# Longer product rows, one unit's place in W_out, a fused bias and maximum, and two sums on GpSimd in a decoder trunk

## The chip, the cores and the metric

The kernel runs on one core of a Trainium2 chip, in one launch. The metric is the device time of an execution in microseconds (us), smaller being better.

## What is computed

A decoder trunk of two layers over 256 tokens of width 1024, in float32. Every layer is a pair of half-step SwiGLU feed-forwards (hidden width 2816) around a token mixer, each with a norm before and after it. The mixer is a gated linear recurrence (width 1344) in the first layer and forgetting attention (16 heads of 64) in the second. Cut to what matters here:

```python
f = swiglu(rms_norm(h, ffn1_pre_g[layer]), ...)          # (silu(x @ w_gate) * (x @ w_up)) @ w_down
h = h + 0.5 * rms_norm(f, ffn1_post_g[layer])
hn = rms_norm(h, mix_pre_g[layer])
m = recurrent_block(hn, ...)                             # ends in  (gelu(gate) * rec) @ w_out
#   or, in the second layer, forgetting_attention:
#   logits = q @ k^T + c[q] - c[k], -inf above the diagonal;  p = softmax(logits);  o = p @ v;  m = o @ w_o
h = h + rms_norm(m, mix_post_g[layer])
f = swiglu(rms_norm(h, ffn2_pre_g[layer]), ...)
h = h + 0.5 * rms_norm(f, ffn2_post_g[layer])
```

Between the layers the shared keys, values and the forget gate's cumulative sum are made from h.

## The kernel before

**Tiles.** The tokens are two tiles t of 128 rows. A float32 number is held as the sum of two numbers of TensorE's faster type, `hi` and `lo`, and a product is three: hi by hi, hi by lo, lo by hi. The weights come from HBM in units of 128 x 1024 (`raw`, 5 buffers, by SyncE's queue). ScalarE copies a unit to `whi` (L204) and VectorE subtracts to get `wlo` (L205); both have 9 buffers.

**Products.** In the feed-forwards' gate and up tiles the weights are stationary and the activations move. `still` and `mmj` work on a row: four PSUM banks by some of the eight blocks of 128 of the contraction. With `whi`, TensorE moves `xhi` and `xlo` side by side, 512 columns (L239, "wide"); with `wlo` it moves `xhi` alone, 256 columns (L245, "narrow"). `grouped` collects units until it gives them to `still`: two units, so 16 wide products and 16 narrow ones, twice for a tile's eight blocks. The other matrices (`row_items`: w_down, W_out, w_o) have the tokens stationary or moving in 512 columns, three products for a unit and half of the output (L212, L213, L214; 6 to a unit). `tick` is called between products; it counts down deferred work (`defer`) and lets the planner load and split further units. `state["edge"]` holds back work that was deferred as calm.

**Order.** TensorE's order is as the program is written. The other engines' instructions stand in the order in which a scheduler put them, each engine in a line of its own; work marked as urgent (`high_priority`) is put forward. W_out has 11 units for each token tile; `OUT_ORDER` says which tile's unit is next.

**Norms and residual.** `enter` takes a finished sub-layer of one token tile in two halves of 512 columns: ScalarE squares each (L260, with a sum `ss` for each half), VectorE multiplies by the gain (L323 or L325), GpSimd adds the two sums and a constant (L253) and takes the power -1/2 (L255), and VectorE multiplies by it and adds h (L329). TensorE then turns h (L269), VectorE multiplies by the next gain (L277), and ScalarE (L278) and VectorE (L283) make `xall` of it. `stat` squares h itself, with one sum. The bfb transfer, `triu` and `ones` (L1051 to L1057) are constants for the forget gate, made by GpSimd when W_out ends.

**Attention.** A step of tile t has a group of heads: 4 for t = 0 (128 keys each), 2 for t = 1 (256 keys each), 512 columns either way; so there are 4 groups and 8. `logits` multiplies q and k (L1198), VectorE adds the bias nb (L1207, in PSUM) and takes each head's negative maximum mx (L1209), ScalarE takes the exponential of each head with its sum (L1215, into `pe` in SBUF), and VectorE divides (L1217, L1218). `turn`, two steps later, transposes pe (L1225), and `values` multiplies by v a step after that (L1239, L1246, L1247).

Of the kernel before, what the change touches and what calls it, by code (L numbers as in the profile page):

```python
# [12 lines left out]
AF = mybir.ActivationFunctionType  # L13
ALU = mybir.AluOpType
AX = mybir.AxisListType

P = 128
D = 1024
# [9 lines left out]
EPS = 1e-6  # L28
# [8 lines left out]
NEG = -1e30  # L37
# [10 lines left out]
def trunk_kernel(ctx: ExitStack, tc: tile.TileContext, A: dict, out: bass.AP):  # L48
    nc = tc.nc
# [11 lines left out]
    def nm(s):  # L61
        uid[0] += 1
        return f"{s}_{uid[0]}"
# [24 lines left out]
    def mmbank():  # L88
        return bank("mm", True)
# [13 lines left out]
    def tensor_work(n):  # L103
        pace["t"] += n * 0.445e-3
# [8 lines left out]
    def tick():  # L113
        for p in list(pend):
            p[0] -= 1
            if p[0] < 0 and not (p[2] and state["edge"]):
                pend.remove(p)
                p[1]()
        purse[0] = min(purse[0] + SHARE, SHARE)
        if state["p"] >= OPEN:  # L120
            prepare_next()
        while queue and purse[0] > 0:
            cost, _, fn = queue.pop(0)
            purse[0] -= cost
            fn()
# [101 lines left out]
    def mmj(bs, parts, ks, moving):  # L227

        o, oh = pall, pall[:, :, :S]
        if len(moving(ks[0])[0].shape) == 4:  # L230
            o = o.rearrange("p n (a t b) -> p n a t b", a=2, t=2)
            oh = oh.rearrange("p n (t b) -> p n t b", t=2)
        else:
            o = o.rearrange("p n (a b) -> p n a b", a=2)
        n = len(ks)
        for i, (k, (wh, wl)) in enumerate(zip(ks, parts)):
            tensor_work(2 * S * len(bs))
            for b, w in zip(bs, wh):
                nc.tensor.matmul(o[:, b], w, moving(k)[0], start=k == 0, stop=False)  # L239
            if n > 1 and i % 2 == 1:  # L240
                tick()
        for i, (k, (wh, wl)) in enumerate(zip(ks, parts)):
            tensor_work(S * len(bs))
            for b, w in zip(bs, wl):
                nc.tensor.matmul(oh[:, b], w, moving(k)[1], start=False, stop=k == 7)  # L245
            if i == 1 and n > 2:
                tick()


    def rstd_of(ss, n, f=1.0):  # L250

        v = spool.tile([P, 1], F32, tag="nv", name=nm("nv"))
        nc.gpsimd.tensor_scalar(v, ss[:, 0:1], ss[:, 1:2] if n == 2 else 0.0, D * EPS * f * f, ALU.add, ALU.add)  # L253
        r = spool.tile([P, 1], F32, tag="rstd", name=nm("rstd"), bufs=8)
        nc.gpsimd.tensor_tensor(r, v, mhalf, ALU.pow)  # L255
        return r
# [125 lines left out]
    state = {"p": 0, "a": 0, "b": 0, "edge": False, "look": 99}  # L382
# [4 lines left out]
    def prepare_next(must=False):  # L387

        i = state["p"]
        if not must and i >= state["a"] + state["look"]:  # L390
            return
        if i >= len(items) or i >= WB and done.get(i - WB, 0) < 2:
            assert not must, i
            return
        if i not in landed:
            landed[i] = max(landed.get(i - 1, 4.0) + LOAD, pace["t"] if i < RAW else split_at[i - RAW] + LATE)
        if landed[i] > pace["t"] and not must:
            return
        pace["t"] = max(pace["t"], landed[i])
        split_at[i] = pace["t"] + 1.0  # L400
        units[i] = items[i][0]()
        state["p"] += 1
# [119 lines left out]
    hooks = {}  # L522
# [23 lines left out]
    def grouped(k0, kept, fn):  # L546

        i = len(items)

        def work(t, u):  # L550
            kept.append((i, u))
            if len(kept) < 2 and not hooks and k0 % 4 == 0:
                return [i]
            us = [v for _, v in kept]
            done_ = [j for j, _ in kept]
            del kept[:]
            fn(us, k0 + 2 - 2 * len(us))
            for j in done_[:-1]:
                done[j] = 2
                units.pop(j)  # L560
        return work
# [444 lines left out]
    for p in range(6):  # L1006
# [1 line left out]
    n_rg = len(items)  # L1008
    RG_ORDER = ("0g0 0g1 0g2 0g3 0g4 0g5 0g6 0g7 1g0 1g1 r0 1g2 r1 gw0 1g3 1g4 r2 gw1 1g5 1g6 r3 gw2 1g7 "
                "0g8 0g9 0g10 r4 gw3 r5 1g8 1g9 gw4 1g10 gw5").split()  # L1010
    OUT_ORDER = [0] * 8 + [1] * 4 + [0] * 3 + [1] * 7

    gbox = {}

# [146 lines left out]
    att = {}  # L1161
# [17 lines left out]
    def attention(t):  # L1179

        ap = pools["a"]
        nk = t + 1
        per = 4 // nk
        np_ = per // 2
        w = nk * P
        box = {}
        G = NH // per

        def head(hg, b, j):
            return 2 * (hg * np_ + j) + b  # L1190

        def logits(hg):
            c = 4 + (hg % 2) * 2
            lg = pall[:, c:c + 2, :S]
            for j in range(np_):
                for b in range(2):
                    p = hg * np_ + j
                    nc.tensor.matmul(lg[:, b, j * w:(j + 1) * w], att["q"][t][b * HD:(b + 1) * HD, p, :],  # L1198
                                     kv["kT"][b * HD:(b + 1) * HD, p, :w], start=True, stop=True)
            v = lg.rearrange("p b (j k) -> p j b k", j=np_)  # L1200
            h0 = hg * per
            bias = att["nb"][t][:, h0:h0 + per, :].rearrange("p (j b) k -> p j b k", b=2)
            if np_ == 1:
                v, bias = lg, att["nb"][t][:, h0:h0 + per, :]
            urgent = tc.high_priority()
            urgent.__enter__()
            nc.vector.tensor_tensor(v, v, bias, ALU.add)  # L1207
            mx = spool.tile([P, 4], F32, tag="mx", name=nm("mx"))[:, :per]
            nc.vector.tensor_reduce(mx, lg.rearrange("p b (j k) -> p b j k", j=np_), AX.X, ALU.max, negate=True)  # L1209
            sm = spool.tile([P, 4], F32, tag="sm", name=nm("sm"))[:, :per]  # L1210
            pe = box["pe", hg] = ap.tile([P, per, w], F32, tag="pe", name=nm("pe"), bufs=2)
            for b in range(2):
                for j in range(np_):
                    i = b * np_ + j
                    nc.scalar.activation(pe[:, i, :], lg[:, b, j * w:(j + 1) * w], AF.Exp, bias=mx[:, i:i + 1],  # L1215
                                         accum_out=sm[:, i:i + 1])
            nc.vector.reciprocal(sm, sm)  # L1217
            nc.vector.tensor_tensor(pe, pe, sm.unsqueeze(2).to_broadcast([P, per, w]), ALU.mult)  # L1218
            urgent.__exit__(None, None, None)

        def turn(hg):
            tp = bank("mm")
            pev = box["pe", hg].rearrange("p a b -> p (a b)")
            for j in range(4):
                nc.tensor.transpose(tp[:, j * P:(j + 1) * P], pev[:, j * P:(j + 1) * P], ident)  # L1225
            pT = box["pT", hg] = ap.tile([P, 4, P], F32, tag="pT", name=nm("pT"), bufs=2)
            nc.scalar.activation(pT.rearrange("p a b -> p (a b)"), tp, AF.Copy)

        def values(hg):
            p0 = hg * np_  # L1230
            if p0 % 2 == 0:
                box["po"] = mmbank()
            po, pT = box["po"], box["pT", hg]
            for j in range(np_):
                o = (p0 + j) % 2 * P
                for k in range(nk):
                    for b in range(2):
                        hd = head(hg, b, j)
                        nc.tensor.matmul(po[b * HD:(b + 1) * HD, o:o + P], kv["v"][k][:, hd * HD:(hd + 1) * HD],  # L1239
                                         pT[:, (b * np_ + j) * nk + k, :], start=k == 0, stop=k == nk - 1)  # L1240
            if (p0 + np_) % 2 == 0:
                k0 = p0 + np_ - 2
                oh_v = att["oh"][t][:, k0:k0 + 2, :].rearrange("p a b -> p (a b)")
                ol_v = att["ol"][t][:, k0:k0 + 2, :].rearrange("p a b -> p (a b)")
                with tc.high_priority():
                    nc.scalar.activation(oh_v, po[:, :S], AF.Copy)  # L1246
                    nc.vector.tensor_tensor(ol_v, po[:, :S], oh_v.bitcast(F32), ALU.subtract)  # L1247
                release(po)

        steps = []  # L1250
        for i in range(G + 3):
            s = []
            if 0 <= i - 3 < G:
                s.append(lambda i=i: values(i - 3))
            if 0 <= i - 2 < G:
                s.append(lambda i=i: turn(i - 2))
            if i < G:
                s.append(lambda i=i: logits(i))
            steps.append(s)
        return steps  # L1260
# [142 lines left out]
    nxt = [n_rg, n_rg]  # L1403
    for t in OUT_ORDER:
        slot(t, nxt[t])
# [66 lines left out]
```

## Time and profile before

| | |
|---|---|
| time, median of 3 runs (lowest, highest) | 988.68 us (988.68, 989.23) |
| profiled execution | 988.85 us |
| its span | 987.1 us |
| TensorE busy | 976.7 us, 99% |
| VectorE, ScalarE, GpSimd busy | 672.8, 567.1, 50.8 us |
| read from HBM | 180.09 MB, 184 GB/s over the span |

The span is from the first instruction to the last; the rest of the execution's time, 1.75 us, lies around it. A row of a timeline is: start in us, duration in us, engine, line, operation, outputs<-inputs, shape; in brackets the time that the engine stood idle before it and what ended that. Operations of one engine overlap in part, so the next one can start before the duration of the last is over; start to start is a step.

### The profile page before, as it was taken

What the parts mean: (1) busy time and instruction counts of PE and PEld (TensorE: products, weight loads), DVE (VectorE), ACT (ScalarE), POOL (GpSimd) and SP (SyncE); (2) the same over time, 40 slices, a digit from 0 to 9 for tenths busy, and PEclk for the clock granted to TensorE, in tenths of its full rate; (3) what the DMA queues carried; (4) which work ended last, traced back from release to release, by engine and by line L of the source; (5) the groups of instructions that cost most, each with busy time, mean ns of one, the idle gap of its engine ahead of it and who ended that gap; (6) DMA issues with size and microseconds to landing.
All of it is one profiled execution on the core that took longest, in us unless ns stands there. A gap on an engine that the chain in (4) does not pass through costs nothing.

```text
span 987.1 us, 13888 instructions
## 1 busy us (share of the span) xinstructions
PE 976.7 (99%) x5294; PEld 836.9 (85%) x5294; DVE 672.8 (68%) x791; ACT 567.1 (57%) x740; POOL 50.8 (5%) x97
## 2 busy tenths in 40 slices
PE   9999999999999999999999999999999999999997
PEld 7888888899988888888898888888887688888885
DVE  5877754668997766664697676764488867667542
ACT  6666543559986655543565555553467665555431
POOL 3300000100003000000000000000030000000000
PEclk9999999999999999999999999999999999999999
DMA  8877546565337766646478666554585157666531
GB/s 276 258 273 228 186 165 191 169 181 159 109 105 230 234 192 186 199 152 179 118 218 273 196 177 192 189 198 162 171 293 177 43 172 236 200 183 193 166 111 43
DMA packets 94088, 182.06 MB, mean 184 GB/s; under 512 B 11822, under 2 KB 33414, under 8 KB 93894
## 3 DMA queue, kind: packets, MB, share of 16 engines
q1 hardware_dynamic: 93350, 181.10, 58.2%
q8 instruction: 41, 0.67, 0.3%
q0 software_dynamic: 640, 0.07, 0.1%
q14 instruction: 25, 0.20, 0.1%
q10 hardware_dynamic: 32, 0.01, 0.0%
HBM read 180.09 MB, written 1.06 MB: 184 GB/s over the span
## 4 chain that ended last, share of the span: by engine, by line
PE 72%; issue 21%; DVE 3%; ACT 3%; POOL 1%; DMA 0%; DVEq 0%; POOLq 0%; SPq 0%; ACTq 0%
PE pall L239 25%; PE pall L245 13%; PE pall L212 9%; PE pall L214 9%; PE pall L213 9%; PE pall L889 1%; PE pall L219 1%; PE pall L220 1%; PE pall L221 1%; DVE wlo L205 1%; PE pall L1198 1%; PE pall L1225 1%; POOL rstd L255 1%; ACT whi L204 0%; ACT junk L260 0%
## 5 line engine op out<-in xcount | busy, mean ns | idle before, releaser
L205 DVE TENSOR_TENSOR wlo<-raw,whi 128x1024 fp32r<-128x1024 f32 (+4 forms) x328 | 389.1, 1206 | 239.3 <-ACT whi L204 114.2
L204 ACT ACTIVATE whi<-raw 128x1024 fp32r<-128x1024 f32 (+4 forms) x328 | 341.0, 1046 | 276.8 <-PE pall L239 128.4
L239 PE MATMUL pall<-xall,whi 128*128 128x512 f32 x1280 | 307.2, 392 | 0.4 <-DVE xall L1322 0.4
L239 PEld LDWEIGHTS pall<-xall,whi 128*128 128x128 f32 x1280 | 235.1, 188 | 46.4 <-DVE xall L1322 0.9
L245 PEld LDWEIGHTS pall<-xall,wlo 128*128 128x128 f32 x1280 | 164.5, 191 | 6.7 <-DVE wlo L1330 0.4
L245 PE MATMUL pall<-xall,wlo 128*128 128x256 f32 x1280 | 167.3, 283 | 0.0
L212 PE MATMUL pall<-whi,hid 128*128 128x512 f32 (+2 forms) x400 | 153.2, 383 | 0.0
L214 PE MATMUL pall<-whi,hid 128*128 128x512 f32 (+2 forms) x400 | 152.6, 382 | 0.3 <-DVE hid L283 0.3
L213 PE MATMUL pall<-wlo,hid 128*128 128x512 f32 (+2 forms) x400 | 152.6, 381 | 0.0
L214 PEld LDWEIGHTS pall<-whi,hid 128*128 128x128 f32 x400 | 75.1, 188 | 14.2 <-DVE hid L283 0.6
L212 PEld LDWEIGHTS pall<-whi,hid 128*128 128x128 f32 x400 | 75.2, 188 | 13.6
L213 PEld LDWEIGHTS pall<-wlo,hid 128*128 128x128 f32 x400 | 75.2, 188 | 13.6
L253 POOL TENSOR_SCALAR nv<-ss 128x1 f32<-128x1 f32 x24 | 10.5, 436 | 922.0 <-ACT junk L260 921.8
L212 PE MATMUL pall<-whi,xall 128*128 128x512 f32 (+2 forms) x144 | 57.3, 398 | 0.0
L214 PE MATMUL pall<-whi,xall 128*128 128x512 f32 (+2 forms) x144 | 55.3, 384 | 0.0
L213 PE MATMUL pall<-wlo,xall 128*128 128x512 f32 (+2 forms) x144 | 55.0, 382 | 0.0
L214 PEld LDWEIGHTS pall<-whi,xall 128*128 128x128 f32 x144 | 27.1, 188 | 5.4 <-DVE xall L283 0.3
L212 PEld LDWEIGHTS pall<-whi,xall 128*128 128x128 f32 x144 | 27.1, 188 | 4.9
L519 ACT ACTIVATE sil<-pall 128x1024 f32<-128x1024 f32 (+1 forms) x22 | 20.9, 949 | 17.9 <-PE pall L245 17.8
L519 ACT ACTIVATE prod<-pall 128x1024 f32<-128x1024 f32 (+1 forms) x22 | 20.8, 948 | 17.7 <-PE pall L245 17.7
L213 PEld LDWEIGHTS pall<-wlo,xall 128*128 128x128 f32 x144 | 27.2, 189 | 4.5
L323 DVE SCALAR_TENSOR_TENSOR t<-pall,rstd,gb 128x512 f32<-128x512 f32 x16 | 11.9, 750 | 26.7 <-ACT junk L260 26.7
(193 smaller groups left out, 978.2 us busy)
## 6 DMA issues: line engine op xcount, KB each, us to landing
raw<-in_ffn_w_down_dram SPq DMA_DIRECT2D x88, 512.0 KB
raw<-in_ffn_w_up_dram SPq DMA_DIRECT2D x80, 512.0 KB
raw<-in_ffn_w_gate_dram SPq DMA_DIRECT2D x78, 512.0 KB
raw<-in_rg_w_in_dram SPq DMA_DIRECT2D x20, 504.0 KB
raw<-in_ffn_w_gate_dram SPq DMA_DIRECT2D x20, 256.0 KB
raw<-in_rg_w_out_dram SPq DMA_DIRECT2D x10, 504.0 KB
raw<-in_ffn_w_up_dram SPq DMA_DIRECT2D x16, 256.0 KB
raw<-in_w_kv_dram SPq DMA_DIRECT2D x8, 512.0 KB
```

What stands on the lines that cost most here:

```text
L204: nc.scalar.activation(hi[:parts, c:c + m], rawv[:, c:c + m], AF.Copy)
L205: nc.vector.tensor_tensor(lo[:parts, c:c + m], rawv[:, c:c + m], hi[:parts, c:c + m].bitcast(F32), ALU.subtract)
L212: nc.tensor.matmul(ps, xh, wh, start=first, stop=False)
L213: nc.tensor.matmul(ps, xh, wl, start=False, stop=False)
L214: nc.tensor.matmul(ps, xl, wh, start=False, stop=last)
L219: nc.tensor.matmul(ps, wh, xh, start=first, stop=False)
L220: nc.tensor.matmul(ps, wh, xl, start=False, stop=False)
L239: nc.tensor.matmul(o[:, b], w, moving(k)[0], start=k == 0, stop=False)
L245: nc.tensor.matmul(oh[:, b], w, moving(k)[1], start=False, stop=k == 7)
L253: nc.gpsimd.tensor_scalar(v, ss[:, 0:1], ss[:, 1:2] if n == 2 else 0.0, D * EPS * f * f, ALU.add, ALU.add)
L323: nc.vector.scalar_tensor_tensor(t1[n], pf[n], r_in, gb[:, n * 512:(n + 1) * 512], ALU.mult, ALU.mult)
L519: nc.scalar.activation(v, pall[:, b:b + m, S:], AF.Copy)
```

## The change

Four parts, in one edit.

1. `grouped` collects all four units of a tile's eight blocks, so that a row is 32 wide products and then 32 narrow ones. `mmj` calls `tick` after every second block, as often per eight blocks as before, and clears `edge` after the second wide pair.
2. `OUT_ORDER` has five units of tile 1 in its second stretch instead of four, and six in its last.
3. GpSimd's sum for the norm is `ss[0] * 1 + constant`; where there are two halves a second instruction adds `ss[1]`.
4. In `logits` each head has one VectorE operation that adds the bias, writes the negated sum to pe in SBUF, and gives the negative maximum; the exponential reads pe with a scale of -1. Each of these operations is two instructions on VectorE, the operation and the read of its result.

```diff
@@ mmj
             if n > 1 and i % 2 == 1:
                 tick()
+                if i > 1:
+                    state["edge"] = False
...
-            if i == 1 and n > 2:
+            if i % 2 == 1 and i < n - 1:
                 tick()
@@ rstd_of
-        nc.gpsimd.tensor_scalar(v, ss[:, 0:1], ss[:, 1:2] if n == 2 else 0.0, D * EPS * f * f, ALU.add, ALU.add)
+        nc.gpsimd.tensor_scalar(v, ss[:, 0:1], 1.0, D * EPS * f * f, ALU.mult, ALU.add)
+        if n == 2:
+            nc.gpsimd.tensor_scalar(v, v, 1.0, ss[:, 1:2], ALU.mult, ALU.add)
@@ grouped
-            if len(kept) < 2 and not hooks and k0 % 4 == 0:
+            if k0 < 6 and not hooks:
                 return [i]
...
-    OUT_ORDER = [0] * 8 + [1] * 4 + [0] * 3 + [1] * 7
+    OUT_ORDER = [0] * 8 + [1] * 5 + [0] * 3 + [1] * 6
@@ logits
-            nc.vector.tensor_tensor(v, v, bias, ALU.add)
...
-            nc.vector.tensor_reduce(mx, lg.rearrange("p b (j k) -> p b j k", j=np_), AX.X, ALU.max, negate=True)
...
                     i = b * np_ + j
-                    nc.scalar.activation(pe[:, i, :], lg[:, b, j * w:(j + 1) * w], AF.Exp, bias=mx[:, i:i + 1],
-                                         accum_out=sm[:, i:i + 1])
+                    nc.vector.tensor_tensor_reduce(pe[:, i, :], lg[:, b, j * w:(j + 1) * w], att["nb"][t][:, head(hg, b, j), :],
+                                                   -1.0, -NEG, ALU.add, ALU.min, mx[:, i:i + 1])
+            for i in range(per):
+                nc.scalar.activation(pe[:, i, :], pe[:, i, :], AF.Exp, bias=mx[:, i:i + 1], scale=-1.0,
+                                     accum_out=sm[:, i:i + 1])
```

The lines behind `mmj` stand two to four later in the changed program (L245 is L247, L253 is L255 and L257, L255 is L259, L260 is L264, L277 is L281, L283 is L287, L325 and L329 are L329 and L333, L1051 to L1057 are L1055 to L1061; the fused operation is L1212).

TensorE, in the first feed-forward, early in the program; whi and wlo are a unit's two parts. Before:

```order
L239 MATMUL pall<-xall,whi_323 128x512 x8
L239 MATMUL pall<-xall,whi_345 128x512 x8
L245 MATMUL pall<-xall,wlo_324 128x256 x8
L245 MATMUL pall<-xall,wlo_346 128x256 x8
L239 MATMUL pall<-xall,whi_359 128x512 x8
L162 MATMUL pall<-ident,grow 128x40
L239 MATMUL pall<-xall,whi_377 128x512 x8
L245 MATMUL pall<-xall,wlo_360 128x256 x8
L245 MATMUL pall<-xall,wlo_378 128x256 x8
```

and in the changed program:

```order
L239 MATMUL pall<-xall,whi_315 128x512 x8
L239 MATMUL pall<-xall,whi_329 128x512 x8
L239 MATMUL pall<-xall,whi_343 128x512 x8
L239 MATMUL pall<-xall,whi_357 128x512 x8
L247 MATMUL pall<-xall,wlo_316 128x256 x8
L162 MATMUL pall<-ident,grow 128x40
L247 MATMUL pall<-xall,wlo_330 128x256 x8
L247 MATMUL pall<-xall,wlo_344 128x256 x8
L247 MATMUL pall<-xall,wlo_358 128x256 x8
```

The narrow products of the first two units went behind the wide ones of the last two.

GpSimd, at the end of W_out; the first rstd is that of h of token tile 0, the second that of W_out's tile 1, nv the sum that it is made from. Before:

```order
L255 TENSOR_TENSOR rstd_2868<-nv_2866,mhalf 128x1
L301 TENSOR_SCALAR rf_2870<-rstd_2868 128x1
L1051 DMA bfb<-in_b_fgate_dram 128x16
L1053 MEMSET triu 128x128
L1057 MEMSET ones 128x128
L1054 AFFINE_SELECT triu<-triu 128x128
L253 TENSOR_SCALAR nv_2929<-ss_2920 128x1
L255 TENSOR_TENSOR rstd_2931<-nv_2929,mhalf 128x1
```

and in the changed program:

```order
L259 TENSOR_TENSOR rstd_2885<-nv_2883,mhalf 128x1
L305 TENSOR_SCALAR rf_2887<-rstd_2885 128x1
L255 TENSOR_SCALAR nv_2934<-ss_2925 128x1
L1055 DMA bfb<-in_b_fgate_dram 128x16
L1057 MEMSET triu 128x128
L1061 MEMSET ones 128x128
L1058 AFFINE_SELECT triu<-triu 128x128
L257 TENSOR_SCALAR nv_2934<-nv_2934,ss_2925 128x1
L259 TENSOR_TENSOR rstd_2937<-nv_2934,mhalf 128x1
```

The new first sum stands ahead of the constants' instructions and the second behind them. In the other norms of two halves the two sums follow one another.

VectorE, in attention of tile 1, where the residual update of tile 0 (t, h) of the sub-layer meets the groups of heads. Before:

```order
L1207 TENSOR_TENSOR pall<-pall,nb_6483 128x2x256
L1217 RECIPROCAL sm_6946<-sm_6946 128x2
L329 SCALAR_TENSOR_TENSOR h<-t_1093_6963,rstd_6969,h 128x512
L1209 TENSOR_REDUCE mx_6988<-pall 128x2
L1218 TENSOR_TENSOR pe_6947<-pe_6947,sm_6946 128x512
L329 SCALAR_TENSOR_TENSOR h<-t_1094_6965,rstd_6969,h 128x512
L1217 RECIPROCAL sm_6990<-sm_6990 128x2
```

and in the changed program:

```order
L1217 RECIPROCAL sm_6962<-sm_6962 128x2
L1218 TENSOR_TENSOR pe_6963<-pe_6963,sm_6962 128x512
L329 TENSOR_TENSOR t_1093_6981<-pall,gb_6648 128x512
L329 TENSOR_TENSOR t_1094_6983<-pall,gb_6648 128x512
L1212 ISA pe_7008,mx_7006<-pall,nb_6493 128x256
L1212 ISA mx_7006 128x1
L1247 TENSOR_TENSOR ol_6504<-pall,oh_6502 128x256
L1212 ISA pe_7008,mx_7006<-pall,nb_6493 128x256
L1212 ISA mx_7006 128x1
L333 SCALAR_TENSOR_TENSOR h<-t_1093_6981,rstd_6988,h 128x512
L333 SCALAR_TENSOR_TENSOR h<-t_1094_6983,rstd_6988,h 128x512
```

The division L1218 of the earlier group (pe_6947 before, pe_6963 now) stood between the two halves of the residual update and now stands ahead of it.

More of the change, by code (lines that the diff above doesn't have):

```diff
@@ L1199, in logits @@
                                      kv["kT"][b * HD:(b + 1) * HD, p, :w], start=True, stop=True)
[L1200 to L1204, printed above, removed]
             urgent = tc.high_priority()
             urgent.__enter__()
-            nc.vector.tensor_tensor(v, v, bias, ALU.add)
             mx = spool.tile([P, 4], F32, tag="mx", name=nm("mx"))[:, :per]
-            nc.vector.tensor_reduce(mx, lg.rearrange("p b (j k) -> p b j k", j=np_), AX.X, ALU.max, negate=True)
             sm = spool.tile([P, 4], F32, tag="sm", name=nm("sm"))[:, :per]
```

## The prediction

> **What bounds the kernel now.** I read the page first (busy time, the slices, the costliest groups), then the waits of TensorE, then the timelines around the places that the change touches. The page says which engine sets the end:
>
> ```profile
> span 987.1 us, 13888 instructions
> PE 976.7 (99%) x5294; PEld 836.9 (85%) x5294; DVE 672.8 (68%) x791; ACT 567.1 (57%) x740; POOL 50.8 (5%) x97
> ...
> PEclk9999999999999999999999999999999999999999
> ...
> L239 PE MATMUL pall<-xall,whi 128*128 128x512 f32 x1280 | 307.2, 392 | 0.4 <-DVE xall L1322 0.4
> ```
>
> TensorE is busy for 99% of the span at the full granted clock. So the time is the sum of its products' steps, plus the few places where it waits. Those are all in one view, the waits of TensorE (released by, total us, times, longest); the rows of interest are:
>
> ```profile
> PE pall L156 <- DVE idle L144: 1.5, 1, 1.5
> PE pall L1225 <- DVE pe L1218: 1.0, 2, 0.7
> ...
> PE pall L214 <- DVE y L974: 0.2, 1, 0.2
> ```
>
> The first is the program's start and is not touched. An edit can therefore gain only by making a product's step shorter, or by removing one of these small waits; it can lose wherever it makes TensorE wait. This bounds the gain to a few us in 987. The profiled execution took 988.85 us (span 987.1 and 1.75 around it), 0.17 above the median of the runs, 988.68. I sum against 988.85 and take 0.17 off at the end. About 0.2%, 1.98 us, is what a measurement of this kernel can tell from no change.
>
> **Part 1, rows of 32 wide and 32 narrow products.** The multiplications are the same ones; only their order changes. TensorE's timeline of a gate and up row (start, us, line):
>
> ```profile
> 336.28 3.82 PE L239 MATMUL pall<-xall,whi 128*128 128x512 f32 x16
> 339.93 2.08 PE L245 MATMUL pall<-xall,wlo 128*128 128x256 f32 x16
> 341.84 2.46 PE L239 MATMUL pall<-xall,whi 128*128 128x512 f32 x10
> ```
>
> and a stretch of 512-wide products that follow one another, with the wait on y in it:
>
> ```profile
> 289.68 0.39 PE L213 MATMUL pall<-wlo,y 126*128 126x512 f32 x1
> ...
> 291.72 0.39 PE L213 MATMUL pall<-wlo,y 126*128 126x512 f32 x1
> 292.35 0.51 PE L214 MATMUL pall<-whi,y 126*128 126x512 f32 x1 [0.24 <-DVE y L974]
> 292.69 0.40 PE L212 MATMUL pall<-whi,y 126*128 126x512 f32 x1
> ```
>
> From 289.68 to 291.72 are nine steps, so a steady step is 0.227 us, and 16 of them 3.63. The wide run after narrow ones took 339.93 - 336.28 = 3.65. A switch costs 0.01 to 0.03 us, with the rounding of the rows. The 1280 wide products are 80 runs of 16 now and 40 of 32 then, so about 40 switches go: 0.4 to 1.2 us, and I take **-0.7**. The last two units of each row are needed earlier by two units' worth of work; the weights' splits (DVE L205, ACT L204) run ahead in a ring of nine buffers, and the waits above show no row that waits for a weight, so I cost that at nothing. If the cover were gone, the wait would be one split, 1.2 us a time.
>
> **Part 2, W_out.** One unit of token tile 1 goes ahead of the last three of tile 0. TensorE's wait on y stood at 292.35: the steps at 291.72 and 292.35 took 0.63 and 0.34 where 0.227 each is normal, so it cost 0.52 us though the wait itself is listed with 0.24. Six products (6 x 0.227 = 1.36 us) now run first, and y is there by then: **-0.5**. Tile 0's residual update moves back by the same six products, and its transposes too, so nothing new waits there.
>
> **Part 3, GpSimd's sums.** Each norm over two halves has one GpSimd instruction more. Fourteen such sums are issued; in thirteen the first one only needs the first Square and is over before the second Square, so the chain keeps its length. The norm of W_out's tile 1 is different: between its two sums now stand the issue of the bfb transfer, two MEMSETs and the AFFINE_SELECT of triu, and GpSimd works in order. Timeline of GpSimd before, with its other 128x128 AFFINE_SELECT, at the start of the program, and one L253 that is as slow as three:
>
> ```profile
> 1.07 0.29 POOL masks.py:199 TENSOR_SCALAR_AFFINE_SELECT ident<-ident 128x128 f32<-128x128 f32 x1
> ...
> 303.58 0.67 POOL L1051 DMA_DIRECT2D bfb<-in_b_fgate_dram  x1 [0.65 <-DVE xg L277]
> 304.56 3.28 POOL L1054 TENSOR_SCALAR_AFFINE_SELECT triu<-triu 128x128 f32<-128x128 f32 x1
> 307.94 0.30 POOL L253 TENSOR_SCALAR nv<-ss 128x1 f32<-128x1 f32 x1
> 308.32 0.57 POOL L255 TENSOR_TENSOR rstd<-nv,mhalf 128x1 f32<-128x1 f32 x1
> ...
> 311.69 1.01 POOL L253 TENSOR_SCALAR nv<-ss 128x1 f32<-128x1 f32 x1 [2.80 <-ACT junk L260]
> ```
>
> VectorE in the same stretch:
>
> ```profile
> 304.12 1.28 DVE L283 TENSOR_TENSOR xall<-xg,xall 128x512 fp32r<-128x512 f32 x2
> 305.33 2.35 DVE L205 TENSOR_TENSOR wlo<-raw,whi 128x1024 fp32r<-128x1024 f32 x2
> 307.60 0.68 DVE L325 TENSOR_TENSOR t<-pall,gb 128x512 f32<-128x512 f32 x1
> ...
> 308.92 1.42 DVE L329 SCALAR_TENSOR_TENSOR h<-t,rstd,h 128x512 f32<-128x512 f32 x2
> 310.25 2.35 DVE L205 TENSOR_TENSOR wlo<-raw,whi 128x1024 fp32r<-128x1024 f32 x2
> ```
>
> The select of 128x128 took 0.29 us alone and 3.28 us here, and it ended 0.24 us after VectorE went from operations with both inputs in SBUF (L283, L205) to L325, which reads PSUM. The L253 at 311.69 ended at 312.70, as the two L205 did (312.60). So I read 3.28 as 0.29 of work and the rest as waiting for VectorE. [...]
>
> What then happens, with ScalarE's and TensorE's rows:
>
> ```profile
> 305.59 0.60 ACT L260 ACTIVATE junk<-pall 128x512 bf16<-128x512 f32 x1
> ...
> 307.16 0.57 ACT L260 ACTIVATE junk<-pall 128x512 bf16<-128x512 f32 x1
> ```
>
> ```profile
> 310.78 1.03 PE L269 MATMUL pall<-ident,h 128*128 128x128 f32 x8
> 311.57 0.48 PE L212 MATMUL pall<-whi,xall 128*128 128x512 f32 x1
> ...
> 317.10 0.61 PE L306 MATMUL pall<-ident,rstd 128*128 128x128 f32 x4
> ```
>
> In these times, the first Square is done at about 306.3 to 306.7 (305.59 + 0.60 and its sum's read; tile 0's later chain pushes it back by up to 1.36, one weight split fewer ahead of it on ScalarE pulls it forward by 1.05). The first sum takes 0.38 (307.94 to 308.32): 307.0. The bfb issue had 0.65 before it and then 0.98 to the select (303.58 to 304.56): the select starts at 308.6, when VectorE has just one split before it comes to L329, where it waits for rstd. With 0.29 it is done at 308.9. Second sum 0.38 and power 0.60 (308.32 to 308.92): L329 starts at 309.9, against 308.92. Its second half ends 1.42 later, at 311.3. TensorE's turn at L269 would be 310.78 - 0.52 (part 2) = 310.26, and its second four transposes would start at 310.66: they start 0.7 late, **+0.7**. The bounds are 0 (all of it 0.7 earlier) and, with the select at its 3.28 again, +3.0 more than that, +3.7. L205 and L277 behind L329 shift by about as much; the next that TensorE needs from there is L306's rstd at 317.10, three us after its making, so nothing else is late.
>
> **Part 4, bias and maximum in one operation.** VectorE's groups by shape in 733 to 800 us, ScalarE's accumulator read, and the stretch in which both are fullest (busy of PE, PEld, DVE, ACT):
>
> ```profile
> L1207 DVE TENSOR_TENSOR pall<-pall,nb 128x512 f32<-128x512 f32 x12 | 8.3, 695 | 4.1 <-PE pall L1198 4.1
> ...
> L1209 DVE TENSOR_REDUCE mx<-pall 128x2 f32<-128x512 f32 x8 | 5.5, 689 | 0.2
> L1247 DVE TENSOR_TENSOR ol<-pall,oh 128x256 fp32r<-128x256 f32 x8 | 3.4, 423 | 3.1 <-ACT oh L1246 3.1
> ...
> L1215 ACT ACTIVATION_READ_ACCUMULATOR pe<-pall,mx 128x1 f32 x32 | 6.6, 207 | 0.0
> ...
> 745.00:755.00 10.00, 9.70 (x64) 6.84 (x63) 9.68 (x16) 9.37 (x26) 0.00 (x0) 1.00 0.78 249
> ```
>
> and the steps of VectorE, start to start:
>
> ```profile
> 777.76 0.42 DVE L1247 TENSOR_TENSOR ol<-pall,oh 128x256 fp32r<-128x256 f32 x1 [0.19 <-ACT oh L1246]
> 778.10 0.68 DVE L325 TENSOR_TENSOR t<-pall,gb 128x512 f32<-128x512 f32 x1
> 778.70 0.69 DVE L1207 TENSOR_TENSOR pall<-pall,nb 128x512 f32<-128x512 f32 x1
> ```
>
> A 512 operation holds VectorE for 0.60 and a 256 one for 0.34; by that slope a 128 one holds it for 0.21, and 0.08 is the part that no element pays for. Before, a group of logits costs 2 x 0.60 = 1.20. The fused operation, and the read of its result as an instruction of its own, are in no row of this trace. At the price of a plain one, with 0.08 for the read, a group of tile 0 costs 4 x 0.29 = 1.16 and one of tile 1 2 x 0.42 = 0.84. With a read of 0.21, as ScalarE's, it is 1.68 and 1.10. I take the first, which is nearest to VectorE's own steps: nothing for tile 0 (4 groups), and 8 x 0.36 = 2.9 us of VectorE's time for tile 1. Only what TensorE waited for comes back:
>
> ```profile
> 752.13 0.66 PE L1225 MATMUL pall<-ident,pe 128*128 128x128 f32 x4 [0.30 <-DVE pe L1218]
> ...
> 781.36 0.66 PE L1225 MATMUL pall<-ident,pe 128*128 128x128 f32 x4 [0.72 <-DVE pe L1218]
> ```
>
> The listed waits are 1.0, and with 0.28 more each, as in the wait on y (0.52 for 0.24), 1.6. At the second, the residual update of tile 0 stood ahead of the product L1218 that it waits for, and in the new order L1218 stands ahead. At the first, the exponentials, which now read SBUF, may hold some of it on ScalarE (9.37 of 10 us). I take **-1.2**. The next wait there would be the values' bank, which no row shows as late.
>
> [...]
>
> **The sum.** -0.7 - 0.5 + 0.7 - 1.2 = -1.7: 988.85 - 1.7 = 987.15 for a profiled execution, and 0.17 less for the median: **987.0**.
>
> **The rivals.**
>
> A, slower: the fused operation is dear. If it runs at half the pace of a plain one, with a read of 0.10, tile 0's group is 4 x 0.52 = 2.1 and tile 1's 2 x 0.78 = 1.56. In 745 to 755 VectorE has 0.32 us free, so the four groups of tile 0 cost 4 x 0.9 - 0.3 = 3.3 there; tile 1 adds 0.36 in two or three of its eight groups, 0.9; and the 1.2 does not come. That is +5.4, 992.4. The time is above 990.7 once an operation of 128 with its read is over 0.48 (4 x 0.72 - 0.3 = 2.6, and the lost 1.2). For it: VectorE is full there. Against: no VectorE row of this trace is that slow for its size. Chance 0.15.
>
> B: the select is 3.28 by itself, or VectorE blocks it as long again. +2.3 to +3.0 on the forecast, 989.3 to 990.0. For it: it is the only triu row. Against: 0.29 for the same shape. Chance 0.12.
>
> C, faster: all that tile 1's groups save (2.9 and not 1.2) is on the path, since the waits return in smaller pieces than the view lists, and the sums of part 3 cost nothing. -1.7 - 0.7: 984.6. Against: TensorE's waits there add up to 1.6 at most. Chance 0.12.
>
> D: a longer wide run keeps the slow start, so part 1 gives nothing: 987.7. Chance 0.08.
>
> **How the numbers follow.** The forecast has 0.53, with a range of its own of 986.0 to 988.3: from -0.5 in part 1, -0.4 in part 4 and -0.1 in part 2 to +0.4, +0.5 and +0.4 in parts 1, 4 and 3. The line for faster lies at 986.7, inside it: I give 0.26 of the 0.53 to faster and 0.27 to the same. With C, faster has 0.38; with B and D, the same has 0.46, less one case of B in ten; slower, A and that, has 0.16. The range takes in C's end and B's, with 0.4 for part 1: 984.6 to 990.4. A alone lies outside.
>
> **What would show it.** In the changed kernel's profile: wide runs of 32 with steps of 0.227 but for the first five; no wait on y; the select of triu short, and L269 late by less than 1 us; on VectorE a group of tile 1 under 1.0 us, and no wait for L1218's product at the two places. The prediction is wrong if TensorE waits longer than 1.5 us for h there, if the fused operation of 128 takes over 0.38 with its read, or if a weight comes late in a row of 32.

## The result, and the profile after

| | before | changed |
|---|---|---|
| median of 16 runs each | 988.75 us | 986.5 us |
| ratio | | 0.9978, 95% interval 0.9972 to 0.9984 |
| span of the profiled execution | 987.1 us | 985.1 us |

The change saves 2.25 us, 0.23%, where 987.0 us and 1.7 saved were forecast. With 16 runs of each the interval is 0.06% either way, finer than the 0.2% that the prediction reckoned with. The page of the changed kernel, busy time:

```profile
span 985.1 us, 13949 instructions
PE 976.4 (99%) x5294; PEld 837.8 (85%) x5294; DVE 664.8 (67%) x831; ACT 565.3 (57%) x740; POOL 54.3 (6%) x111
```

TensorE still sets the time. VectorE is busy for 8.0 us less in spite of 40 more instructions. The waits of TensorE, all of them:

```profile
PE pall L156 <- DVE idle L144: 1.5, 1, 1.5
PE pall L214 <- DVE hid L287: 0.3, 1, 0.3
PE pall L367 <- DVE hn L360: 0.3, 1, 0.3
```

The two waits for L1218's product and the wait for y are gone. One more row of before is missing, a wait of 0.4 for xall at 6 us, which the prediction did not show. That is no gain: TensorE's first transposes ran slower here, before

```profile
4.77 0.60 PE L1316 MATMUL pall<-ident,h 128*128 128x128 f32 x4
```

and in the changed kernel

```profile
4.80 1.06 PE L1316 MATMUL pall<-ident,h 128*128 128x128 f32 x4
```

and the product that started at 18.7 us before started 0.40 later. No part touches the start of the program, and it differs among the traces below as well, also in kernels that begin as the one before does; why stays open.

TensorE's timeline of a gate and up row, the 32 wide products and the narrow ones behind them:

```profile
341.54 7.44 PE L239 MATMUL pall<-xall,whi 128*128 128x512 f32 x32
348.82 3.40 PE L247 MATMUL pall<-xall,wlo 128*128 128x256 f32 x27
```

32 wide products took 348.82 - 341.54 = 7.28 us, and 32 steps of 0.2267 (the nine steps of the prediction, 2.04 us) are 7.25. The switch costs its 0.02 to 0.03 us as before, but once for 32.

GpSimd, then VectorE, at the end of W_out:

```profile
306.25 0.19 POOL L255 TENSOR_SCALAR nv<-ss 128x1 f32<-128x1 f32 x1 [2.46 <-ACT junk L264]
307.14 0.66 POOL L1055 DMA_DIRECT2D bfb<-in_b_fgate_dram  x1 [0.70 <-DVE t L329]
...
308.11 0.31 POOL L1058 TENSOR_SCALAR_AFFINE_SELECT triu<-triu 128x128 f32<-128x128 f32 x1
308.41 0.26 POOL L257 TENSOR_SCALAR nv<-nv,ss 128x1 f32<-128x1 f32 x1
308.75 0.57 POOL L259 TENSOR_TENSOR rstd<-nv,mhalf 128x1 f32<-128x1 f32 x1
```

```profile
306.84 1.21 DVE L205 TENSOR_TENSOR wlo<-raw,whi 128x1024 fp32r<-128x1024 f32 x1
...
309.36 1.42 DVE L333 SCALAR_TENSOR_TENSOR h<-t,rstd,h 128x512 f32<-128x512 f32 x2 [0.71 <-POOL rstd L259]
```

The select of triu took 0.31 us, where it had taken 3.28: it began when the split (L205) was over. VectorE waits 0.71 us for rstd, and TensorE's eight transposes show what comes through:

```profile
310.16 1.32 PE L273 MATMUL pall<-ident,h 128*128 128x128 f32 x8
311.24 0.48 PE L212 MATMUL pall<-whi,xall 128*128 128x512 f32 x1
```

From the first transpose to the next product are 1.08 us, where it was 0.79 (310.78 to 311.57); with the step into the first transpose the difference is 0.35. In attention, VectorE's fused operation (count, busy us, mean ns):

```profile
L1212 DVE CUSTOM_DVE_ANT_0 pe<-pall,nb 128x256 f32<-128x256 f32 x16 | 6.2, 420 | 5.4 <-PE pall L1202 5.3
L1212 DVE CUSTOM_DVE_ANT_0 pe<-pall,nb 128x128 f32<-128x128 f32 x16 | 3.7, 285 | 3.0 <-PE pall L1202 3.0
```

### The profile page after: what moved, and what is told of

Same layout as the page of the kernel before. It is cut to its first block, busy times and chain, and to the rows that moved or that the text cites. A ratio compares the mean times of both kernels' runs of the same rounds, so it can differ in the third digit from the quotient of the medians.

```text
span 985.1 us, 13949 instructions
## 1 busy us (share of the span) xinstructions
PE 976.4 (99%) x5294; PEld 837.8 (85%) x5294; DVE 664.8 (67%) x831; ACT 565.3 (57%) x740; POOL 54.3 (6%) x111
## 4 chain that ended last, share of the span: by engine, by line
PE 97%; DVE 1%; issue 1%; ACT 0%; POOL 0%; POOLq 0%; DVEq 0%; ACTq 0%
PE pall L239 31%; PE pall L247 16%; PE pall L212 14%; PE pall L214 13%; PE pall L213 13%; PE pall L893 2%; PE pall L219 1%; PE pall L221 1%; PE pall L220 1%; PE pall L1202 1%; PE pall L1239 1%; PE pall L1225 1%; PE pall L273 1%; PE pall L156 0%; ACT junk L264 0%
## 5 line engine op out<-in xcount | busy, mean ns | idle before, releaser
L205 DVE TENSOR_TENSOR wlo<-raw,whi 128x1024 fp32r<-128x1024 f32 (+4 forms) x328 | 384.5, 1205 | 215.2 <-ACT whi L204 121.8
L239 PE MATMUL pall<-xall,whi 128*128 128x512 f32 x1280 | 300.3, 391 | 0.0
L239 PEld LDWEIGHTS pall<-xall,whi 128*128 128x128 f32 x1280 | 237.9, 189 | 47.9 <-DVE xall L1322 0.7
L247 PEld LDWEIGHTS pall<-xall,wlo 128*128 128x128 f32 x1280 | 159.7, 192 | 3.6
L247 PE MATMUL pall<-xall,wlo 128*128 128x256 f32 x1280 | 161.2, 283 | 0.0
L255 POOL TENSOR_SCALAR nv<-ss 128x1 f32<-128x1 f32 x24 | 12.7, 528 | 903.5 <-ACT junk L264 903.5
L639 DVE TENSOR_TENSOR hid<-prod,hid 128x1024 fp32r<-128x1024 f32 (+1 forms) x22 | 24.8, 1128 | 25.3 <-ACT hid L638 25.3
```

The lines of the kernel that those rows point to most:

```text
L205: nc.vector.tensor_tensor(lo[:parts, c:c + m], rawv[:, c:c + m], hi[:parts, c:c + m].bitcast(F32), ALU.subtract)
L255: nc.gpsimd.tensor_scalar(v, ss[:, 0:1], 1.0, D * EPS * f * f, ALU.mult, ALU.add)
L639: nc.vector.tensor_tensor(lv, pv, hv.bitcast(F32), ALU.subtract)
```

## The experiments

The theory was that of the prediction: each part has its own place on TensorE's path and its own few tenths, and the parts add up. Its rivals stand with each run. The first four kernels are the kernel before with one part of the change alone.

**Part 1 alone** (the edits in `mmj` and `grouped`).

> Part 1 alone on the kernel before: rows of 32 wide and 32 narrow products, nothing else changed. Theory (each change from narrow to wide costs 0.01 to 0.03 us, and about 40 of them go): 0.4 to 1.2 us less, spread evenly over the four feed-forwards, with a wide run of 32 showing slow steps only in its first five. Rival (the slow start grows with the run): no change. Rival (a weight comes late in a row of 32): a new wait of TensorE on a weight, 1 us or more longer.

Measured: 987.68 against 988.7, ratio 0.999 (0.9981 to 0.9999). TensorE's waits are those of before:

```profile
PE pall L1227 <- DVE pe L1220: 1.0, 2, 0.7
...
PE pall L214 <- DVE y L976: 0.3, 1, 0.3
```

No weight comes late, and a row's steps are as in the changed kernel: 0.23 to 0.24 us for the first five wide products, 0.227 from then on. But the switches are not the whole gain. One wide run of before took 3.94 us from start to start (75.88 to 79.82), where one usually takes 3.65. A weight load of TensorE (PEld) waited there for `par`, which VectorE copied from PSUM behind a weight split. That wait is in the list of the weight loads' waits, and not in TensorE's own list. TensorE's row, the wait, and VectorE's rows before:

```profile
75.88 4.10 PE L239 MATMUL pall<-xall,whi 128*128 128x512 f32 x16
...
PEld pall L239 <- DVE par L744: 0.4, 1, 0.4
...
75.07 1.23 DVE L205 TENSOR_TENSOR wlo<-raw,whi 128x1024 fp32r<-128x1024 f32 x1 [2.21 <-issue]
76.22 0.24 DVE L744 COPY par<-pall 126x88 f32<-126x88 f32 x1
```

With part 1 VectorE's order is the other way round, and no weight load waits for `par`:

```profile
75.19 0.24 DVE L746 COPY par<-pall 126x88 f32<-126x88 f32 x1
75.35 1.22 DVE L205 TENSOR_TENSOR wlo<-raw,whi 128x1024 fp32r<-128x1024 f32 x1
```

Start to start, that wait was worth 0.28 us, and the switches that go (82 runs of 16 became 41 of 32) 0.02 each, 0.8 in all. So the gain is not spread evenly over the feed-forwards, as the theory had it: 0.52, 0.15, 0.27 and 0.15, with the wait in the first and more rows in the third. By the time alone the size would be uncertain: its interval reaches from 0.1 to 1.9.

**Part 2 alone.**

```diff
-    OUT_ORDER = [0] * 8 + [1] * 4 + [0] * 3 + [1] * 7
+    OUT_ORDER = [0] * 8 + [1] * 5 + [0] * 3 + [1] * 6
```

> Part 2 alone: one unit of tile 1 of W_out earlier. Theory: the wait on y and its 0.52 us go, and nothing else becomes late: 0.5 us less, all of it at 292 us of the trace. Rival (tile 0's chain, six products later, is late at its own transposes): no change or up to 0.8 longer.

Measured: 988.34 against 988.7, ratio 0.9996 (0.9987 to 1.0005), so the time alone can't tell it from nothing. The waits can: the one on y is gone and none has come. At that place the trace gains 0.52 us start to start, the amount forecast.

```profile
PE pall L1225 <- DVE pe L1218: 1.0, 2, 0.7
...
PE pall L214 <- DVE hid L283: 0.3, 1, 0.3
```

**Part 3 alone** (the edit in `rstd_of`).

> Part 3 alone: two sums on GpSimd. GpSimd's order around triu is the one of the changed kernel, but here two weight splits of VectorE stand ahead of the residual update and not one. Theory (GpSimd's reads and VectorE's operations with two SBUF inputs exclude one another; the select itself is 0.3): the first sum waits for the second split until 307.6, the select then runs in 0.3 while VectorE waits, L329 starts 1.5 to 2.2 us late, and the time is 1.2 to 2.0 longer. Rival (the select takes 3.3 by itself): L329 5 us late, 4 or more longer. Rival (no stall at all): no change.

Measured: 989.27 against 988.7, ratio 1.0005 (0.9996 to 1.0014): 0.6 longer, which the interval can't tell from nothing, and well under the 1.2 expected. GpSimd's and VectorE's timelines:

```profile
306.78 1.44 POOL L253 TENSOR_SCALAR nv<-ss 128x1 f32<-128x1 f32 x1 [3.42 <-ACT junk L262]
308.26 0.66 POOL L1053 DMA_DIRECT2D bfb<-in_b_fgate_dram  x1
...
309.23 0.31 POOL L1056 TENSOR_SCALAR_AFFINE_SELECT triu<-triu 128x128 f32<-128x128 f32 x1
```

```profile
305.80 2.36 DVE L205 TENSOR_TENSOR wlo<-raw,whi 128x1024 fp32r<-128x1024 f32 x2
...
310.48 1.41 DVE L331 SCALAR_TENSOR_TENSOR h<-t,rstd,h 128x512 f32<-128x512 f32 x2 [1.12 <-POOL rstd L257]
```

The mechanism is the one expected. The first sum, which took 0.19 in the changed kernel, took 1.44 here and ended at 308.22, as the two splits did (308.16); the select then took 0.31. Two things were wrong in the forecast of the time. The bfb issue followed the sum at once (308.22 to 308.26), so the 0.65 that I had put between them was not paid; that its own waits had been worked off while the sum stood is a guess. L331 waited 1.12 us. And without part 2 about 0.8 us of such a delay is slack: before, the second half of h was ready at 310.34 and its transposes' turn came at 311.18. TensorE's transposes took 1.07 from first to next product (311.29 to 312.36), 0.28 more than before, 0.37 with the step into the first. The rival by which the select takes 3.3 itself is ruled out.

**Part 4 alone** (the edit in `logits`).

> Part 4 alone: bias and maximum in one operation for each head. Theory (only the two waits on L1218's product come back): 1.2 us less, within 1.0 to 1.6, though VectorE is busy for about 8 us less. Rival (VectorE's time is on the path): 2.9 less or more. Rival (the gain needs the other parts): under 0.5.

Measured: 987.82 against 988.7, ratio 0.9991 (0.9982 to 0.9999): 0.9 less. VectorE:

```profile
PE 976.6 (99%) x5294; PEld 836.3 (85%) x5294; DVE 667.3 (68%) x831; ACT 569.6 (58%) x740; POOL 51.7 (5%) x97
```

It is busy for 5.5 us less than before, and about one of them comes back: both waits for L1218's product are gone, 0.37 and 0.79 us start to start, and TensorE's times move nowhere else in this trace by more than 0.02. So VectorE's time as such is not on the path. What moved is its order. The third group of heads, whose product TensorE waited for at 752, before:

```profile
744.37 0.69 DVE L1207 TENSOR_TENSOR pall<-pall,nb 128x512 f32<-128x512 f32 x1
744.97 1.22 DVE L205 TENSOR_TENSOR wlo<-raw,whi 128x1024 fp32r<-128x1024 f32 x1
746.10 0.68 DVE L1209 TENSOR_REDUCE mx<-pall 128x4 f32<-128x512 f32 x1
...
751.39 0.68 DVE L1218 TENSOR_TENSOR pe<-pe,sm 128x512 f32<-128x512 f32 x1
```

and here, with no split between the bias and the maximum:

```profile
746.13 0.68 DVE L1214 TENSOR_TENSOR pe<-pe,sm 128x512 f32<-128x512 f32 x1
```

The product comes 5 us earlier, by far more than the fused operations save.

**The change without part 3.** Parts 1, 2 and 4 on the kernel before.

> The changed kernel without part 3, so with one sum for each norm and no instruction of GpSimd between. Theory (the first sum ahead of triu still costs about 0.3 us at the transposes of W_out's tile 1): 0.3 us less than the changed kernel, 986.2, and the eight transposes L269 at 310 us take 0.8 from first to last and not 1.1. Rival (GpSimd's sums cost nothing): the same as the changed kernel, 986.5. Rival (two instructions are shorter than one with two scalars): longer.

Measured: 985.9 against 988.91, ratio 0.9971 (0.9961 to 0.9982), the fastest of all kernels here. Its transposes:

```profile
309.93 1.03 PE L271 MATMUL pall<-ident,h 128*128 128x128 f32 x8
310.71 0.48 PE L212 MATMUL pall<-whi,xall 128*128 128x512 f32 x1
```

0.78 from first to next product: the 0.3 that part 3 costs there are gone. GpSimd's select of triu took 1.01 us here, beside two VectorE operations with both inputs in SBUF (on xall, L285 in this kernel):

```profile
305.28 1.01 POOL L1056 TENSOR_SCALAR_AFFINE_SELECT triu<-triu 128x128 f32<-128x128 f32 x1
```

That this kernel is faster than the whole change by 0.6 us isn't shown by the two intervals, which overlap. Of the traces' difference 0.36 lies at these transposes and 0.08 at the norm at 496 us; both go with part 3, so it brings nothing and costs about 0.4.

**GpSimd against VectorE.** The changed kernel and, for GpSimd:

```diff
     run_ffn(ffn_b)
+    probe = spool.tile([P, P], F32, tag="probe", name="probe", bufs=1)
+    nc.gpsimd.memset(probe, 1.0)
+    for _ in range(32):
+        nc.gpsimd.affine_select(out=probe, in_=probe, compare_op=ALU.is_ge, fill=0.0, base=0, ...)
+    for _ in range(32):
+        nc.gpsimd.memset(probe, 1.0)
```

> The changed kernel with 32 selects of 128x128 in place and then 32 MEMSETs of the same tile on GpSimd in a stretch where VectorE alternates between operations with two SBUF inputs and others; the tile isn't used. Theory (exclusion): a select beside an idle VectorE or one that reads PSUM takes 0.3 us, one that meets a VectorE operation with two SBUF inputs ends 0.1 to 0.3 us after that operation's end, and no MEMSET is stretched. Rival (a select is slow for reasons of its own): long ones without such an operation beside them. Of the time nothing is concluded; VectorE may be held up in turn.

The scheduler put them into the first feed-forward. The durations of the probe tile's instructions (min, median, max in ns), and two selects with the VectorE operation beside the first (the second has none):

```profile
L1417 POOL TENSOR_SCALAR_AFFINE_SELECT probe<-probe x32: 292/1157/1242, 33.5 to 60.2; 128x128 f32<-128x128 f32 x32
L1420 POOL MEMSET probe<- x32: 204/205/209, 60.6 to 68.7; 128x128 f32 x32
```

```profile
45.47 1.16 POOL L1417 TENSOR_SCALAR_AFFINE_SELECT probe<-probe 128x128 f32<-128x128 f32 x1
48.29 0.29 POOL L1417 TENSOR_SCALAR_AFFINE_SELECT probe<-probe 128x128 f32<-128x128 f32 x1
```

```profile
45.23 1.26 DVE L205 TENSOR_TENSOR wlo<-raw,whi 128x1024 fp32r<-128x1024 f32 x1
```

The same instruction takes 0.29 beside an idle VectorE and 1.16 beside a split, and ends at 46.63, 0.14 after the split (46.49). So it is with all 32: the 18 long ones (up to 1.24 us) each end about 0.15 after a VectorE operation with two SBUF inputs (41.85 behind 41.70, 40.62 behind 40.46), and the 14 of 0.29 stand beside none, beside one that reads PSUM, or start ahead of one. None of the 32 MEMSETs, which read nothing, is over 0.21, and the changed kernel's MEMSET of triu took 0.23 (from 307.80) beside the split that ran until 308.05. VectorE is held up by less: one of its operations with two SBUF inputs took up to 1.31 us beside these selects, where the changed kernel, without them, has 1.22.

**VectorE's time or its order.** Two kernels put back into each group the VectorE time that part 4 saved. The first has an operation of 384 columns ahead of the fused ones:

```diff
+            nc.vector.tensor_tensor(pe.rearrange("p a b -> p (a b)")[:, :384]..., lg[:, :, :192], ..., ALU.add)
             for b in range(2):
                 for j in range(np_):
```

> The changed kernel with one more VectorE operation of 384 columns ahead of each group's fused ones (its result is overwritten), so that a group costs VectorE about 1.2 us again, as before the change. L1218's product still stands ahead of the residual update's second half. Theory (the gain of part 4 comes from that order, not from VectorE's time): within 0.3 us of the changed kernel, 986.5, and no wait for L1218's product. Rival (it comes from the time): the two waits return, 1.2 us longer, 987.7.

Measured: 989.93 against 988.91, ratio 1.001 (1.0001 to 1.0019): 3.4 longer than the changed kernel, more than either theory or rival. The waits that are new:

```profile
PE pall L1226 <- DVE pe L1219: 2.0, 2, 1.1
...
PE pall L212 <- DVE t L329: 0.7, 1, 0.7
```

They stand at 752 and 789 us, and at 780, and cost 1.14, 1.03 and 1.01 us start to start. The experiment is confounded: the scheduler put weight splits, and once the product with the gain (L329), between this operation and the fused ones, so the maxima came later than by the operation's own 0.5 us. The second kernel has the same operation behind the fused ones, on a bank that nobody reads any more:

```diff
+            nc.vector.tensor_tensor(lg[:, :, :192], lg[:, :, :192], ..., ALU.add)
             nc.vector.reciprocal(sm, sm)
```

> The changed kernel with one more VectorE operation of 384 columns in each group, behind the fused ones and written to the group's dead PSUM bank, so it adds VectorE time (about 1.2 us a group again) and is not on the way to the maxima and exponentials. Most L1218 products keep their place. Theory (VectorE's time counts only where it pushes L1218 past TensorE's turn, so in the two full stretches at 745 to 755 and 775 to 785): 0 to 1.2 us longer than the changed kernel, 986.5 to 987.7. Rival (the earlier pad's 3.4 us are VectorE's time as such): 3 us longer again, 989.5.

Measured: 987.52 against 988.87, ratio 0.9987 (0.9978 to 0.9996), 1.0 longer than the changed kernel. There is one wait for that product again, not two and not twelve:

```profile
PE pall L1226 <- DVE pe L1219: 1.1, 1, 1.1
```

and VectorE is busy for 670.5 us, 5.7 more than in the changed kernel. The wait is at 787 us, for the twelfth group, which had no wait before. Its product in the changed kernel, and here, behind the operations on xg (L281):

```profile
783.12 0.69 DVE L1218 TENSOR_TENSOR pe<-pe,sm 128x512 f32<-128x512 f32 x1
```

```profile
785.04 1.28 DVE L281 TENSOR_TENSOR xg<-pall,gT 128x512 f32<-128x512 f32 x2
786.24 0.68 DVE L1219 TENSOR_TENSOR pe<-pe,sm 128x512 f32<-128x512 f32 x1
```

The first kernel's wait at 789 is for the same group, with the same change of order. The tenth group's, the one at 781 before, came back in neither kernel. So the forecast of the first kernel failed, but its theory is not refuted: wherever a wait came, the order of VectorE's work had changed too. The rival, time as such, falls with the second: 5.7 us more of VectorE's time cost one wait. Both kernels changed the time and the order at once, so the two are not separated.

**Part 4 in halves.** The kernel before with the fused operation for one tile only (`if t == 0:` or `if t == 1:` around the new code, the old in the other branch).

> The kernel before with the fused operation only for tile 0's four groups. VectorE's order in tile 1's groups is the one before. Theory (each of the two waits belongs to its own tile's groups): the wait at 752 goes and the one at 781 stays: 0.4 us less, 988.4. Rival (both go with VectorE's time): 1.2 less. Rival (tile 0's groups gain nothing, as their operations are as many microseconds): no change.

> The kernel before with the fused operation only for tile 1's eight groups, where L1218 of the sixth group moves ahead of the residual update. Theory: the wait at 781 goes and the one at 752 stays: 0.8 us less, 988.0. Rival: 1.2 less or no change.

Measured: tile 0 alone 988.56 against 988.87 (ratio 0.9998, 0.9989 to 1.0007), tile 1 alone 988.33 (0.9996, 0.9987 to 1.0005). The times are inside the intervals, but the waits are plain. Tile 0 fused:

```profile
PE pall L1240 <- DVE pe L1233: 0.7, 1, 0.7
```

and tile 1 fused:

```profile
PE pall L1240 <- DVE pe L1233: 0.3, 1, 0.3
```

Each half takes away its own wait, listed with 0.3 or 0.7, and leaves the other as it was; start to start that gains 0.37 and 0.79.

**Product by product.** All kernels issue 5294 products of TensorE (transposes counted), so the start of one and the same product can be compared between two traces. The table says by how many us each stretch got longer (+) or shorter (-) than in the kernel before, one trace for each kernel; the stretches go by the times of before:

| stretch | 0 to 19 | to 289 | to 334 | to 493 | to 502 | to 664 | to 818 | to 980 |
|---|---|---|---|---|---|---|---|---|
| what the change meets there | start | feed-forward 1 | W_out | feed-forward 2 | a norm | feed-forward 3 | attention | feed-forward 4 |
| part 1 | -0.11 | -0.52 | +0.06 | -0.15 | +0.01 | -0.27 | -0.01 | -0.15 |
| part 2 | +0.05 | +0.04 | -0.56 | 0.00 | +0.02 | -0.01 | -0.02 | 0.00 |
| part 3 | +0.43 | +0.04 | +0.38 | -0.01 | +0.10 | 0.00 | -0.03 | 0.00 |
| part 4 | -0.01 | +0.02 | -0.02 | 0.00 | +0.02 | -0.01 | -1.16 | 0.00 |
| all four | +0.40 | -0.52 | -0.19 | -0.15 | +0.08 | -0.28 | -1.17 | -0.16 |

Each part moves its own places only, within 0.06. Behind the start, the parts alone add up to -2.25 and the whole change to -2.39. The start is not theirs: in the two kernels with one half of part 4, which begin as the kernel before does, it is 0.17 and 0.28 earlier.

## Why the prediction was right

The time alone says little: the stated range, 984.6 to 990.4, took in rivals B, C and D as well. The parts say more.

- **Part 1**, forecast -0.7: -1.0 alone. The mechanism is shown for 0.8 of it (41 switches of 0.02, one slow start for 32, no weight late). The other 0.28 is the weight load's wait for `par`, which went by a new order of VectorE that nobody planned. The prediction held that all of TensorE's waits are in one view; this one was not.
- **Part 2**, forecast -0.5: -0.4 alone, 0.52 at its place in the trace. The wait on y went, and nothing took its place.
- **Part 3**, forecast +0.7: the transposes cost 0.35 more, and a norm at 496 us, where the prediction had nothing, 0.08. The reading of the 3.28 us as 0.3 of work and the rest as waiting for VectorE was right, and it decided between 987 and 989.3 or more. The term was too large in its first steps: the first Square let the sum start at 306.25, where I took 306.6, and the sum held GpSimd for 0.19, not 0.38. So L333 started at 309.36, not 309.9.
- **Part 4**, forecast -1.2: -0.9 alone, -1.16 in the trace, and both waits gone. That the size fits so well is partly luck: the prediction took the waits to be worth 0.28 more each than listed (1.6) and then some off for ScalarE. They were worth 0.07 more each, and nothing was left for ScalarE to hold up. For the second wait it named the cause, the order of L1218 and the residual update. For the first it named none; what the runs show is the split that no longer stands between bias and maximum. The price was wrong on the safe side. A 128 operation with its read was put at 0.29 and a 256 one at 0.42 a step; the timeline of the changed kernel has them start 0.21 and 0.35 apart, with the read under the next operation:

```profile
742.86 0.29 DVE L1212 CUSTOM_DVE_ANT_0 pe<-pall,nb 128x128 f32<-128x128 f32 x1
743.07 0.08 DVE L1212 DVE_READ_ACCUMULATOR2_ANT mx<- 128x1 f32 x1
743.07 0.29 DVE L1212 CUSTOM_DVE_ANT_0 pe<-pall,nb 128x128 f32<-128x128 f32 x1
```

  So a group of tile 0 saves 0.36 where nothing was forecast (4 x 0.21 against 1.20), and nearly all that VectorE saves is off the path, as forecast.
- **The rivals.** A needed over 0.48 for a 128 operation with its read: 0.21. B needed a long select: 0.31. C needed VectorE's time on the path: 5.5 us saved and 0.9 gained (1.16 in the trace). D needed the slow start to grow: 7.28 for 32. Nor did the number of VectorE's instructions decide: for a group of tile 0 eight (4 x 0.21) are cheaper here than two (2 x 0.60).
- **The sum.** The four parts alone give -1.0 - 0.4 + 0.6 - 0.9 = -1.7, the whole -2.25. Each of these has an interval of about 0.9 us either way, so the times alone do not show that they add up. The traces do: behind the start, -2.25 for the parts and -2.39 for the whole.

What stays open: in the kernel before, the select of triu stood behind four VectorE operations in turn (two L283, two L205; 3.28 us), and without part 3 behind two (1.01), while each select of the probe stood behind one only (1.24 at most). What lets GpSimd in between two VectorE operations in one case and not in the other wasn't tried.

## What to carry to other kernels

In a kernel whose bottleneck engine is 99% busy, list that engine's waits and take from an edit elsewhere only what these rows can give back: 5.5 us of VectorE's time were worth about 1, namely the two waits that a new order of VectorE's work removed. List the waits of the weight loads as well: 0.28 us stood only there. Before a long instruction's duration is carried to another place, look at what ran beside it: the same select is 0.3 or 3.3 us. And when one instruction becomes two on one engine, read what the scheduler has put between them.

## What was not expected of the hardware

- The read of a fused operation's result cost VectorE no step of its own: 83 ns long, it lay under the next operation, and 128 columns went every 0.21 us.
- GpSimd's small sum took 0.19 us beside an operation that reads PSUM, and 1.44 when two splits ran (part 3 alone): here the neighbours, not the work, set the duration.
- A wait's listed size was not its worth: the listed 0.24, 0.30 and 0.72 gave back 0.52, 0.37 and 0.79 us when they went.
